# Seven products in one more place of a two-layer trunk, a pair of steps moved back by one, and a scaling deferred

## The chip, the cores and the metric

The kernel runs on one core of one Trainium2 chip. The metric is device time of one execution in microseconds (us). Three runs of the kernel before took 2038.50, 2039.89 and 2045.22 us, median 2039.89. The profiled execution is a separate one.

## The reference

Two layers over 256 tokens of width 2048, all in float32. Cut to what matters here:

```python
for l in range(DEPTH):                                   # 2 layers
    h = rms_norm(x, norm1_g[l]);  z = h @ w_in[l]        # 2048 -> 5120
    ...                                                  # 8 attention heads, 8 gated groups -> mix
    x = x + mix @ w_out[l]                               # 2048 -> 2048
    h2 = rms_norm(x, norm2_g[l])
    x = x + square(relu(h2 @ w_up[l])) @ w_down[l]       # 2048 -> 8192 -> 2048
return rms_norm(x, final_g)
```

The change touches only the last product of a layer, with `w_down`, and its result's way back to x.

## The kernel before

**Splitting.** A float32 product is made of three matmuls. Every weight tile arrives by DMA as `raw`; ScalarE (ACT) rounds it to `hi` (line 167), VectorE (DVE) makes `lo = raw - hi` (line 177). The activations are split in the same way (`to_half`, lines 640 and 643). TensorE (PE) then adds hi x hi, hi x lo and lo x hi.

**Steps.** The whole program is a list of steps, each with its weight units, its matmuls and what follows. An ordinary step (`transposed`, lines 400 to 404) takes one unit of 512 x 256 weights and issues 24 matmuls of 256 columns. The emission loop (lines 993 to 1014) goes through the list; `done` counts units, and at each step ACT is given the `hi` of units up to six ahead of `done`, VectorE the `lo` of units up to five ahead, then the step's matmuls are issued. Each engine works its own instructions in this order.

**The MLP in eighths.** The hidden width of 8192 is cut into eighths of 1024. The loop over e (lines 902 to 922) lines up, for e = 0 to 8, the sixteen ordinary steps of the up product of eighth e and then the steps of the down product of eighth e-1. The text calls one turn of it block e. The hidden values are squared without the norm's factor for e below 7; the results are scaled by the squared factor (`n2.r2`, `n2.R2`) when they go back into x.

**Seven products.** For some groups of 512 output columns the down product is done as two steps of `fast` instead of four ordinary steps: a 2 x 2 block product with seven multiplications in place of eight. One such step has four weight units: Top, Bottom, and two Sums, which VectorE makes in place from the raw tiles (lines 218, 219, 222, 223). It has 36 matmuls (lines 430, 432, 433) of six products; the seventh product's six matmuls are left over and go behind the third matmul of the next ordinary step. The step also needs sums of the hidden values: `sums` (lines 796 to 799 on VectorE) and four `parts`, each split by ACT and VectorE (lines 640, 643 with the tile `shared`), queued behind the last up step of the eighth. `sums_ready` issues what is still missing of them ahead of the step's matmuls. The seven accumulators of group 0 stay in PSUM (tile `aux`) over the blocks; those of groups 1 and 2 are copied out by ACT (lines 897, 883) and added up in DRAM by DMAs that POOL issues (`put`, line 862; tile `far`). In the last block of a group (`FINAL`) they come back, `combine` adds them to the four quarters on VectorE, ACT scales these by `n2.r2` (line 825), `turn_back` transposes them on TensorE (line 835), and `update` adds them to x (line 499).

**Order.** `ORDER` and `USUAL` give for each block and group the two indices among the block's ordinary steps ahead of which the two seven-product steps stand. `soon(n, fn)` calls fn at the first step at which `done` is n units further; `later` puts work into a queue of which each step takes about 1.2 units of cost. In block 1 today only groups 0 and 1 use seven products, at indices 7, 10 and 13, 14; the third group's columns (1024 to 1535) are four ordinary steps there, and `after_down` adds them to x directly (lines 761 and 499). In blocks 2 to 6 group 1 stands at 1, 2, group 2 at 6, 7 and group 0 at 11, 14.

Of the kernel before, what the change touches and what calls it, by code (L numbers as in the profile page):

```python
# [31 lines left out]
AF = mybir.ActivationFunctionType  # L32
OP = mybir.AluOpType
# [26 lines left out]

ORDER = {1: ((7, 10), (13, 14)), 7: ((6, 9), (1, 2)), 8: ()}
FINAL = (7, 7, 6)
LAST = (4, 6, 8, 10, 0, 2, 12, 14)
USUAL = ((11, 14), (1, 2), (6, 7))
WARM = 11
HALVES = 5
D_SCORES, D_NORM, D_TURN, D_VALUES = 2, 1, 3, 2
# [21 lines left out]
def trunk(ctx: ExitStack, tc: tile.TileContext, layout, xT, consts, gains, w, b_sp, w_sp, out):  # L91
    nc = tc.nc
# [10 lines left out]
    vec, act, pe = nc.vector, nc.scalar, nc.tensor  # L103
# [142 lines left out]
    def soon(delay, fn):  # L246

        due.append((now[0] + delay, fn))
# [258 lines left out]
    def layer(l, n1, n2, n3, last):  # L507
# [218 lines left out]
        d = 0  # L726
        if l == 0:
            d = 9
# [27 lines left out]
        def after_down(e, c, ps):  # L756

            if e == 8:
                update(n3, c, ps, True, last)
            elif c < 12:  # L760
                vec.tensor_tensor(pair(ps), pair(ps), wide(n2.R2), op=OP.mult)
                update(n3, c, ps, False, last)
            elif e == 1:
                act.activation(rest_sums[:, c - 12:c - 10, :], pair(ps), AF.Copy)
            else:
                y = rest_sums[:, c - 12:c - 10, :]
                vec.tensor_tensor(y, y, pair(ps), op=OP.add)
# [40 lines left out]
        def combine(place, c, banks, o=None):  # L808

            d1, d2, d3, d5, d7, d6, d4 = (place[:, 256 * n:256 * (n + 1)] for n in range(7))  # L810
            p1, p2, p3, p5, p7, p6, p4 = o or (d1, d2, d3, d5, d7, d6, d4)
            if o:
                act.activation(d1, p1, AF.Copy)
            vec.tensor_tensor(d2, d1, p2, op=OP.add)
            vec.tensor_tensor(d6, d1, p6, op=OP.add)
            vec.tensor_tensor(d7, d6, p7, op=OP.add)
            vec.tensor_tensor(d6, d6, p5, op=OP.add)
            vec.tensor_tensor(d3, d6, p3, op=OP.add)
            vec.tensor_tensor(d4, d7, d4, op=OP.subtract)
            if o:  # L820
                vec.tensor_tensor(d4, d4, p4, op=OP.subtract)
            vec.tensor_tensor(d7, d7, p5, op=OP.add)
            for tt, out in enumerate(((d2, d3), (d4, d7))):
                for d in out:
                    act.activation(d, d, AF.Copy, scale=n2.r2[:, tt:tt + 1])
            wait = 6 if o else 7
            soon(wait, lambda: turn_back(c, d2, d4, banks[0]))
            soon(wait + (1 if o else 2), lambda: turn_back(c + 2, d3, d7, banks[1]))

        def turn_back(c, first, second, bank):  # L830
            ps = bank()
            for j in range(2):
                for tt, src in enumerate((first, second)):
                    o = j * S + tt * P
                    pe.transpose(ps[:, o:o + P], src[:, j * P:(j + 1) * P], ident)
            soon(1, lambda: update(n3, c, ps, False, last))
# [20 lines left out]
        far = [dp.tile([P, 256 if g == 0 else 7 * 256], F32, name=f"far{l}{g}") for g in range(3)]  # L857

        def put(e, g, r):

            src = stage[:, r] if g else stage_one
            nc.gpsimd.dma_start(far[g][:, r], src, **({} if e == max(g, 1) else {"accum_op": OP.add}))  # L862

        def seventh_out(e, o):
            act.activation(stage_one, o[6], AF.Copy)  # L865
            put(e, 0, slice(0, 256))

        def first_done(e):
            def f(o):
                if e < 7:  # L870
                    soon(5, lambda: seventh_out(e, o))
                else:
                    soon(10, lambda: nc.gpsimd.dma_start(stage[:, 1536:1792], far[0]))
                    soon(14, lambda: combine(stage, 0, [aux_bank] * 2, o))
                    for i, c in enumerate((12, 14)):
                        soon(17 + 2 * i, lambda c=c: rest_in(c))
            return f

        def other_done(e, g, banks):
            here = [lambda i=i: acc_bank(i) for i in (2, 3)]  # L880

            def rest(o):
                act.activation(stage[:, 1536:1792], o[6], AF.Copy)
                for i in range(4):
                    soon(2 * i, lambda r=slice(512 * i, min(512 * (i + 1), 1792)): move(r))
                if e == FINAL[g]:
                    soon(9, lambda: combine(stage, 4 * g, here))

            def move(r):
                if e < FINAL[g]:  # L890
                    put(e, g, r)
                else:
                    nc.gpsimd.dma_start(stage[:, r], far[g][:, r], accum_op=OP.add)

            def f(o):
                for i in (2, 0, 1):
                    act.activation(stage[:, 512 * i:512 * (i + 1)], banks[i], AF.Copy)
                soon(5, lambda: rest(o))
            return f

        base = len(steps)
        for e in range(9):
# [3 lines left out]
            if e:  # L906
                w = 512 * len(ORDER.get(e, USUAL))
                hidden = [hid[e - 1]]
                down = collect(transposed, "w_down", l, (e - 1) * 1024, 8, w, D - w, from_tiles(hidden, NH),
                               lambda c, ps, e=e, w=w: after_down(e, (c + w) // P, ps),  # L910
                               apart=last and e == 8, of=2 if e < 8 else 4,
                               cols=None if e < 8 else [c * P for c in LAST])
                for g, at in enumerate(ORDER.get(e, USUAL)):
                    banks = []
# [107 lines left out]
    for c, w in [(0, 1), (1, 1)] + [(c, 2) for c in range(2, KC, 2)]:  # L1022
        r = slice(c, c + w)
# [38 lines left out]
```

## Time and profile before

| what | value |
|---|---|
| median of three runs | 2039.89 us (2038.50 to 2045.22) |
| profiled execution, its own time | 2044.94 us |
| its span, first to last instruction | 2042.6 us |
| granted TensorE clock, mean | 0.998 |
| TensorE matmul busy | 2027.5 us (99%), 16834 matmuls |
| VectorE busy | 1579.3 us (77%) |
| ScalarE busy | 1214.8 us (59%) |
| GpSimd busy | 156.8 us (8%) |

A matmul's end is modelled in the profile, so the busy share of TensorE doesn't tell how densely matmuls are issued; the number of matmuls in equal stretches does. L402 is line 402 of the kernel; `out<-in` names the tiles that an instruction writes and reads, and a bracket behind a row gives the idle time of the engine before it and what ended it.

### The profile page before, as it was taken

The page shows a single profiled execution, that of the slowest core. Times are in us where ns is not written, and L with a number is a line of the kernel's source. Part 1 is how long each engine was busy: PE and PEld are TensorE (multiplying, and loading weights), DVE is VectorE, ACT ScalarE, POOL GpSimd, SP SyncE. Part 2 cuts the span into 40 slices and gives each one's busy share as a digit, 9 for nine tenths or more (in the row PEclk, how much of TensorE's full clock was granted, in tenths as well). Part 3 has the DMA queues.
Part 4 walks back from the last instruction along what each step waited for, and adds up shares of the span by engine and source line. Part 5 has one row for each costly group of instructions (what it writes and reads, how often), then busy time and mean ns, then how long its engine had stood idle before and what let it go on. Part 6 is the DMA issues. An engine that isn't in the chain of part 4 may idle for free.

```text
span 2042.6 us, 40747 instructions
## 1 busy us (share of the span) xinstructions
PE 2027.5 (99%) x16834; PEld 1988.6 (97%) x16834; DVE 1579.3 (77%) x1950; ACT 1214.8 (59%) x1613; POOL 156.8 (8%) x200
## 2 busy tenths in 40 slices
PE   9999999999999999999999999999999999999997
PEld 8998999999999999999989989999999999999997
DVE  7566765788888888888855667667888888888985
ACT  7565455666675665765545554556665766667654
POOL 0002300001010010100000023000010100100000
PEclk9999999999999999999999999999999999999999
DMA  9555556567586776865565555555676866868562
GB/s 326 191 166 167 184 193 203 168 233 220 196 260 206 227 220 193 241 214 202 197 216 172 169 176 191 191 191 178 217 231 199 272 190 216 256 197 259 184 217 84
DMA packets 126442, 419.26 MB, mean 205 GB/s; under 512 B 14128, under 2 KB 22064, under 8 KB 126256
## 3 DMA queue, kind: packets, MB, share of 16 engines
q1 hardware_dynamic: 110800, 389.86, 56.3%
q0 software_dynamic: 14304, 23.86, 6.4%
q8 instruction: 131, 2.15, 0.4%
q10 hardware_dynamic: 1152, 2.94, 0.4%
q14 instruction: 55, 0.45, 0.1%
HBM read 394.58 MB, written 22.02 MB: 204 GB/s over the span
## 4 chain that ended last, share of the span: by engine, by line
PE 91%; DVE 5%; ACT 2%; issue 1%; DMA 1%; ACTq 0%; DVEq 0%; SPq 0%
PE acc L402 22%; PE acc L404 22%; PE acc L400 22%; PE acc L461 3%; PE acc L459 3%; PE acc L460 3%; PE aux L430 3%; PE aux L433 3%; PE aux L432 3%; PE acc L430 2%; PE acc L432 2%; PE acc L433 2%; DVE lo L177 2%; ACT hi L167 1%; DVE shared L643 1%
## 5 line engine op out<-in xcount | busy, mean ns | idle before, releaser
L167 ACT ACTIVATE hi<-raw 128x1024 fp32r<-128x1024 f32 (+1 forms) x817 | 836.8, 1050 | 516.2 <-DVE raw L219 233.9
L177 DVE TENSOR_TENSOR lo<-raw,hi 128x1024 fp32r<-128x1024 f32 (+1 forms) x817 | 965.0, 1213 | 155.8 <-ACT hi L167 153.6
L400 PE MATMUL acc<-hs,hi 128*128 128x256 f32 x2816 | 784.4, 279 | 0.0
L402 PE MATMUL acc<-hs,lo 128*128 128x256 f32 x2816 | 782.5, 278 | 0.4
L404 PE MATMUL acc<-hs,hi 128*128 128x256 f32 x2816 | 781.3, 277 | 0.0
L402 PEld LDWEIGHTS acc<-hs,lo 128*128 128x128 f32 x2816 | 529.2, 188 | 2.7 <-DVE lo L177 2.0
L400 PEld LDWEIGHTS acc<-hs,hi 128*128 128x128 f32 x2816 | 530.8, 189 | 0.4 <-issue 0.2
L404 PEld LDWEIGHTS acc<-hs,hi 128*128 128x128 f32 x2816 | 529.0, 188 | 0.0
L400 PE MATMUL acc<-half,hi 128*128 128x256 f32 x1344 | 373.0, 278 | 2.3 <-ACT hi L167 2.3
L402 PE MATMUL acc<-half,lo 128*128 128x256 f32 x1344 | 372.0, 277 | 0.0
L404 PE MATMUL acc<-half,hi 128*128 128x256 f32 x1344 | 372.0, 277 | 0.0
L400 PEld LDWEIGHTS acc<-half,hi 128*128 128x128 f32 x1344 | 252.8, 188 | 2.6 <-ACT hi L167 2.6
L402 PEld LDWEIGHTS acc<-half,lo 128*128 128x128 f32 x1344 | 252.6, 188 | 0.0
L404 PEld LDWEIGHTS acc<-half,hi 128*128 128x128 f32 x1344 | 252.4, 188 | 0.0
L862 POOL DMA_DIRECT2D far<-ar x92 | 74.7, 983 | 1168.2 <-ACT ar L865 620.7
L432 PE MATMUL acc<-lo,shared 128*128 128x256 f32 x384 | 107.4, 280 | 0.0
L433 PE MATMUL acc<-hi,shared 128*128 128x256 f32 x384 | 106.6, 277 | 0.0
L430 PE MATMUL acc<-hi,shared 128*128 128x256 f32 x384 | 106.5, 277 | 0.0
L643 DVE TENSOR_TENSOR half<-ar,half 128x512 fp32r<-128x512 f32 x72 | 49.7, 691 | 67.8 <-ACT half L640 67.6
L459 PE MATMUL acc<-hi,hs 128*128 128x512 f32 x256 | 101.7, 397 | 0.0
L461 PE MATMUL acc<-hi,hs 128*128 128x512 f32 x256 | 100.7, 393 | 0.0
L460 PE MATMUL acc<-lo,hs 128*128 128x512 f32 x256 | 100.0, 390 | 0.5 <-DVE lo L177 0.5
(163 smaller groups left out, 2563.3 us busy)
## 6 DMA issues: line engine op xcount, KB each, us to landing
raw<-in_w SPq DMA_DIRECT2D x731, 512.0 KB, 4.6
far<-ar POOLq DMA_DIRECT2D x60, 256.0 KB, 7.4
far<-ar POOLq DMA_DIRECT2D x32, 128.0 KB, 5.1
ar<-far POOLq DMA_DIRECT2D x12, 256.0 KB, 8.6
raw<-in_w SPq DMA_DIRECT2D x10, 256.0 KB, 4.8
x<-in_xT SPq DMA_DIRECT2D x7, 256.0 KB, 6.0
out<-x SPq DMA_DIRECT2D x7, 256.0 KB, 3.1
shared<-in_b_sp ACTq DMA_DIRECT2D x2, 512.0 KB, 7.7
```

Source lines behind the costliest of these rows:

```text
L167: act.activation(self.h[:, j * m:(j + 1) * m], self.raw[:, j * m:(j + 1) * m], AF.Copy)
L177: vec.tensor_tensor(lo[:, r], self.raw[:, r], self.h[:, r].bitcast(F32), op=OP.subtract)
L400: pe.matmul(o, lhsT=hi, rhs=xs[:, 0, :], start=(k0 + k == 0 and (two or cb == 0)), stop=False, skip_group_check=True)
L402: pe.matmul(o, lhsT=wt.lo[:, k, cb * P:(cb + 1) * P], rhs=xs[:, 0, :], start=False, stop=False, skip_group_check=True)
L404: pe.matmul(o, lhsT=hi, rhs=xs[:, 1, :], start=False, stop=last, skip_group_check=True)
L430: pe.matmul(o[n], lhsT=xh, rhs=hi, start=(p == 0 and k == 0 and n in fresh), stop=False, skip_group_check=True)
L432: pe.matmul(o[n], lhsT=xh, rhs=lo, start=False, stop=False, skip_group_check=True)
L433: pe.matmul(o[n], lhsT=xl, rhs=hi, start=False, stop=(n in last and p == 1 and k == 1), skip_group_check=True)
L459: pe.matmul(ps, lhsT=xh, rhs=hi, start=(k0 + k == 0), stop=False)
L460: pe.matmul(ps, lhsT=xh, rhs=lo, start=False, stop=False)
L461: pe.matmul(ps, lhsT=xl, rhs=hi, start=False, stop=(k0 + k == KC - 1))
L862: nc.gpsimd.dma_start(far[g][:, r], src, **({} if e == max(g, 1) else {"accum_op": OP.add}))
```

## The change

Three places change. `ORDER` loses its entry for block 1, which then follows `USUAL`: three groups use seven products there, with the pair of group 1 at 2, 3, that of group 2 at 6, 7 and that of group 0 at 11, 14. In `USUAL` and in block 7 the pair of group 1 moves from 1, 2 to 2, 3. The scaling in `combine` is no longer issued right behind VectorE's sums but by `soon(3, ...)`. With group 2 starting in block 1, `put` copies in block 1 and adds in all later ones, for every group.

```diff
-ORDER = {1: ((7, 10), (13, 14)), 7: ((6, 9), (1, 2)), 8: ()}
+ORDER = {7: ((6, 9), (2, 3)), 8: ()}
 FINAL = (7, 7, 6)
 LAST = (4, 6, 8, 10, 0, 2, 12, 14)
-USUAL = ((11, 14), (1, 2), (6, 7))
+USUAL = ((11, 14), (2, 3), (6, 7))
...
             vec.tensor_tensor(d7, d7, p5, op=OP.add)
-            for tt, out in enumerate(((d2, d3), (d4, d7))):
-                for d in out:
-                    act.activation(d, d, AF.Copy, scale=n2.r2[:, tt:tt + 1])
+
+            def scale():
+                for tt, out in enumerate(((d2, d3), (d4, d7))):
+                    for d in out:
+                        act.activation(d, d, AF.Copy, scale=n2.r2[:, tt:tt + 1])
+
+            soon(3, scale)
             wait = 6 if o else 7
...
-            nc.gpsimd.dma_start(far[g][:, r], src, **({} if e == max(g, 1) else {"accum_op": OP.add}))
+            nc.gpsimd.dma_start(far[g][:, r], src, **({} if e == 1 else {"accum_op": OP.add}))
```

## The prediction

> **What bounds the kernel now.** I read the page's first lines, then the waits of the weight load, then equal stretches of TensorE, then single matmuls where the stretches differ.
>
> ```profile
> span 2042.6 us, 40747 instructions
> PE 2027.5 (99%) x16834; PEld 1988.6 (97%) x16834; DVE 1579.3 (77%) x1950; ACT 1214.8 (59%) x1613; POOL 156.8 (8%) x200
> ...
> PEld acc L400 <- ACT hi L167: 2.6, 2, 1.3
> PEld acc L402 <- DVE lo L177: 2.0, 8, 0.3
> ```
>
> TensorE issues a matmul all the time, and its waits on others sum to a few us (the last two rows: total, times, longest). So the time is the number of matmuls times their spacing, plus few waits. The spacing has two values (columns: stretch, its length, then busy us and count of each engine, granted clock, DMA):
>
> ```profile
> 562.00:635.00 73.00, 73.00 (x644) 73.00 (x643) 62.64 (x72) 48.73 (x62) 7.54 (x9) 1.00 0.74 228
> 646.00:719.00 73.00, 73.00 (x623) 73.00 (x622) 61.06 (x70) 47.16 (x61) 7.39 (x9) 1.00 0.73 225
> 719.00:792.00 73.00, 73.00 (x623) 73.00 (x623) 60.92 (x65) 47.21 (x60) 7.89 (x9) 1.00 0.82 251
> 792.00:865.00 73.00, 73.00 (x624) 73.00 (x622) 64.84 (x78) 46.81 (x61) 7.08 (x8) 1.00 0.68 206
> 904.50:939.00 34.50, 34.50 (x295) 34.50 (x294) 32.09 (x39) 23.40 (x30) 3.55 (x4) 1.00 0.81 258
> ...
> 1661.00:1734.00 73.00, 73.00 (x644) 73.00 (x643) 62.75 (x72) 48.53 (x62) 7.23 (x9) 1.00 0.74 228
> ```
>
> (Block e is a turn of the loop over e, lines 902 to 922: the up product of eighth e and the down product of eighth e-1.) The same mix of work puts 644 matmuls into 73 us in one block (113.4 ns each) and 623 in another (117.2 ns) at the same granted clock of 1.00. I call them the quick and the slow rhythm. The slow one fills about 644 to 883 and 904 to 945 in layer 0, 280 us together, and costs 280/73 x 21 x 0.1134 = 9.1 us of this execution. Where does it begin? At waits in the seven-product steps (single matmuls: start, duration):
>
> ```profile
> 641.54 0.28 PE L433 MATMUL acc<-hi,shared 128*128 128x256 f32 x1
> 641.65 0.28 PE L430 MATMUL acc<-hi,shared 128*128 128x256 f32 x1
> 641.81 0.39 PE L432 MATMUL acc<-lo,shared 128*128 128x256 f32 x1
> 642.04 0.28 PE L433 MATMUL acc<-hi,shared 128*128 128x256 f32 x1
> ...
> 643.80 0.28 PE L433 MATMUL acc<-hi,shared 128*128 128x256 f32 x1
> 643.92 0.28 PE L400 MATMUL acc<-hs,hi 128*128 128x256 f32 x1
> 644.24 0.39 PE L402 MATMUL acc<-hs,lo 128*128 128x256 f32 x1
> 644.47 0.28 PE L404 MATMUL acc<-hs,hi 128*128 128x256 f32 x1
> ...
> 557.96 0.39 PE L432 MATMUL acc<-lo,shared 128*128 128x256 f32 x1
> ...
> 1909.60 0.39 PE L432 MATMUL acc<-lo,shared 128*128 128x256 f32 x1
> ...
> 1657.05 0.28 PE L433 MATMUL acc<-hi,shared 128*128 128x256 f32 x1
> ...
> 1658.75 0.28 PE L433 MATMUL acc<-hi,shared 128*128 128x256 f32 x1
> ```
>
> Ahead of 641.65 the starts lie 0.11 apart. The L432 of the fourth product waits for its low part, and from 642.04 to 643.80, 15 matmuls on, they lie 0.117 apart: the wait left the step in the slow rhythm. Eight such waits stand inside a seven-product step (the first and the last are the rows at 557.96 and 1909.60). Seven left it slow; the one at 1656.8 did not (1657.05 to 1658.75 is 0.113 each). Here a second wait follows at the ordinary step behind (643.92 to 644.47), and after most of these second waits the rhythm is quick again; after this one it wasn't. Once ordinary steps run slow, seven-product steps that end without a wait do not end it: the two slow stretches hold eighteen of them. Both ended where turned-back products are transposed:
>
> ```profile
> L835 PE MATMUL acc<-con,ar x32: 271/273/274, 876.4 to 1953.3; 128*128 128x128 f32 x32
> ```
>
> **Matmuls.** Per layer block 1 loses four ordinary steps of 24 matmuls and gains two seven-product steps of 42: 12 fewer, 24 in both layers, x 0.1134 = **-2.7 us**. VectorE gets, per new step, three low parts of 1.22, one of 0.68 and four sums of 0.69 (7.1 us beside 42 x 0.1134 = 4.8 us of TensorE), and loses per layer four low parts and the four operations that scaled and added columns 8 to 11 to x.
>
> ```profile
> L177 DVE TENSOR_TENSOR lo<-raw,hi 128x1024 fp32r<-128x1024 f32 x807 | 958.4, 1220 | 151.9 <-ACT hi L167 149.7
> L190 DVE TENSOR_TENSOR lo<-raw,hi 128x512 fp32r<-128x512 f32 x76 | 52.0, 684 | 1.3 <-ACT hi L185 1.3
> L218 DVE TENSOR_TENSOR raw<-raw 128x512 f32<-128x512 f32 x76 | 52.0, 684 | 0.0
> L862 POOL DMA_DIRECT2D far<-ar x92 | 74.7, 983 | 1168.2 <-ACT ar L865 620.7 <-ACT ar L897 436.7 <-ACT ar L883 110.8
> ```
>
> So 14.2 - 4.9 - 2.8 = 6.5 us more on VectorE in a block of 83 us; the blocks that already do this keep it 62.64 of 73 us busy. On average it is hidden; where it isn't comes next. POOL issues four more transfers a layer (0.98 us each), and those of block 2 add instead of copy; POOL idles 1168 us ahead of this line and the next access to the same place is a block later: nothing. Uncovered, they would be 8 us on POOL's own queue, on which nothing of TensorE waits.
>
> **The new first pair.** In block 1 the first pair now sits behind the second ordinary step instead of the seventh. Between it and the last up step of block 0, whose output the sums are made of, no down steps lie. The order in which VectorE gets its work up to the third step is by the code the same as before, so its rows of today hold:
>
> ```profile
> 379.79 0.69 DVE L643 TENSOR_TENSOR half<-ar,half 128x512 fp32r<-128x512 f32 x1 [2.35 <-ACT half L640]
> 380.52 0.69 DVE L796 TENSOR_TENSOR ar<-ar 128x512 f32<-128x512 f32 x1
> ...
> 384.44 1.28 DVE L643 TENSOR_TENSOR shared<-ar,shared 128x512 fp32r<-128x512 f32 x2
> 385.64 1.22 DVE L177 TENSOR_TENSOR lo<-raw,hi 128x1024 fp32r<-128x1024 f32 x1
> 386.78 1.28 DVE L643 TENSOR_TENSOR shared<-ar,shared 128x512 fp32r<-128x512 f32 x2
> ...
> 377.63 0.28 PE L400 MATMUL acc<-hs,hi 128*128 128x256 f32 x1
> ...
> 383.07 0.28 PE L400 MATMUL acc<-hs,hi 128*128 128x256 f32 x1
> ...
> 384.66 0.28 PE L404 MATMUL acc<-hs,hi 128*128 128x256 f32 x1
> ```
>
> Block 1's first step starts at 377.63, its third at 383.07: there the pair's first step will start. Its first two products (12 matmuls) need only the hidden tile; the third reads the low part of sum rows 4 and 5, at matmul 14, that is 384.66. VectorE makes that part in the first half of the row at 386.78, done 387.4. TensorE waits **2.8 us**, in both layers (layer 1 has the same rows 1015.0 us later): **+5.6 us**. Queued behind it are only matmuls, and VectorE uses the pause to get ahead, so the second of the pair follows without one. Bounds: 0, if the parts were made in another order; 3.4, if the step waits for the last part (the row's end, 388.06).
>
> **The later pair elsewhere.** Blocks 3 to 6 now wait twice around the pair: 0.05 + 0.12 inside it and 0.21 + 0.11 behind it by the rows from 641.65 to 644.47, 0.49 together. One ordinary step more ahead of the pair gives 24 x 0.1134 = 2.72 us for 1.22 us of VectorE, 1.5 us of lead, more than the 0.49: gone in six such places (blocks 3 and 4 of layer 0, whose 5 and 6 ran slow and had none, and four in layer 1): **-2.9 us**. The pair's evacuation by ACT and its four transfers on POOL follow a step later, and SP loads the same tiles in the new order; POOL is idle and seven raw buffers stand between: nothing. The next pair keeps its place; work and time ahead of it are unchanged in sum, so its lead stays. In block 7 VectorE works without a pause up to the other pair, so a wait removed early can come back there: between 0 and 1.3 us, I take **-0.6**.
>
> **The scaling.** ACT now stands before it while VectorE combines; the question is whether TensorE feels it.
>
> ```profile
> L825 ACT ACTIVATE ar<-ar,nr 128x256 f32<-128x256 f32 x24 | 10.9, 500 | 9.1 <-DVE ar L814 5.1 <-DVE ar L818 3.4 <-DVE ar L821 0.6
> ...
> 970.14 0.69 DVE L761 TENSOR_TENSOR acc<-acc,nR 128x512 f32<-128x512 f32 x1
> 970.87 0.69 DVE L499 TENSOR_TENSOR x<-x,acc 128x512 f32<-128x512 f32 x1
> ...
> 970.28 0.28 PE L404 MATMUL acc<-half,hi 128*128 128x256 f32 x1
> 971.70 0.36 PE L400 MATMUL acc<-half,hi 128*128 128x256 f32 x1 [1.15 <-ACT hi L167]
> ```
>
> TensorE's longest wait after the start is here, 1.3 us in each layer. The row blames ACT, but this matmul opens a bank which VectorE's L499 has to free, and that ends at 971.56. The combine's sums stay ahead of it, so deferring ACT's scaling changes nothing: **0**. If the row is right, -2.6. A loss needs the scaling to come too late for the transposes: it still has at least one ordinary step (2.72 us) for its four operations (2.0 us).
>
> **What follows the new wait.** It is a wait inside a seven-product step, like the eight, and no wait comes at the step behind it to mend the rhythm. By those rows it runs slow, and stays slow up to the transposes late in block 6 (876.4 today). A block has 20 x 24 + 6 x 42 = 732 matmuls, 732 x 3.8 ns = 2.8 us; 0.9 of block 1, four whole ones and 0.9 of block 6 make 16.2 us a layer, **+32.4**. Bounds: 0 and 32.4. I take the upper, by seven of eight. The Trainium skill (TensorE: Matmul & The Clock Gate, "Step-by-step: what each phase is for") says that loading the next weights takes no read bandwidth from the running matmul; by it a wait would cost its own length and no more. The 623 against 644 matmuls disagree, though they don't show why. That rule's result is the first rival below.
>
> Sum, on the profiled execution's 2044.94 us (span 2042.6): -2.7 + 5.6 - 2.9 - 0.6 + 0 - 9.1 (today's slow stretches, begun by waits that go) + 32.4 = **2067.6 us**. The median of the runs, 2039.89, lies 5 us under the profiled execution; without a slow rhythm today's kernel would take 2035.8, so I read the median as 4 us of it. Against the median the forecast is 1.4% slower.
>
> **Rivals.** *The rhythm stays quick* behind the new wait: 2067.6 - 32.4 = 2035.2. For it: the one quick case in eight, and that the wait is far longer than those. Against: the other seven. *One layer only* goes slow: 2051.4; the same kernel shows both rhythms in layer 0 and only the quick one in layer 1, so chance decides. *On the other side, the new pair does not wait*: it is decided by whether the low part of sum rows 4 and 5 lands by 384.6 rather than 387.4. VectorE stands idle 2.35 us ahead of 379.79, so there is room; but the row after must wait for the last up step, and then nothing is idle. Then neither wait nor slow rhythm: 2035.2 - 5.6 = 2029.6, 0.5% faster. *The change of ACT's order does what I deny*, with a quick rhythm: 2035.2 - 2.6 = 2032.6.
>
> **How the numbers follow.** What a measurement can tell from no change is 0.3%, 6.1 us: 2033.8 to 2046.0. Forecast 0.38, one layer 0.16, quick rhythm 0.18 (two thirds of it inside the 0.3%, the rest faster), no wait 0.15, ACT's order 0.09, something slower of another kind 0.04. Faster: 0.15 + 0.09 + 0.06 = 0.30; same 0.12; slower 0.58. The range goes from 2031 (leaving out the no-wait case) to 2071 (the longer wait and no gain at the pairs); the forecast's own range is 2060 to 2071.
>
> **What would show it.** Right: a TensorE wait near 2.8 us in the third product after two ordinary steps of block 1, ended by VectorE's L643, in both layers; 623 matmuls per 73 us from there to the transposes; none of the 0.1 to 0.3 us waits for L177 at the pair in later blocks; 16810 matmuls; the 1.3 us wait in the last down block but one still there. Wrong: 644 matmuls per 73 us after that wait, or no wait.

## The result, and the profile after

The changed kernel takes 2058.36 us (median of 4 runs, 2055.94 to 2058.51) beside 2039.2 us for the kernel before on the same chip: 1.0088 times as long (the ratio is taken over all runs, not of the medians), 95% interval 1.0072 to 1.0103. The forecast was 1.4% slower: 2067.6 us for the profiled execution, which took 2058.51, below the forecast's own range of 2060 to 2071. Sign and first cause are as predicted. Most of the difference is lost at steps that the prediction had counted as unchanged or as a small gain, and its largest term, a slow rhythm behind the new wait, is missing.

The page of the changed kernel (first lines: span, then busy us, share and count of each engine) and its waits of TensorE (total, times, longest):

```profile
span 2056.7 us, 40733 instructions
PE 2030.9 (99%) x16810; PEld 1986.4 (97%) x16810; DVE 1593.3 (77%) x1966; ACT 1225.9 (60%) x1629; POOL 163.7 (8%) x208
...
PE acc L402 <- DVE lo L177: 5.7, 14, 1.3
PE acc L433 <- DVE shared L643: 4.0, 2, 2.0
...
PE acc L430 <- ACT shared L640: 0.8, 2, 0.4
```

TensorE has the 24 matmuls fewer that the diff promises (16834 before), and three waits that the kernel before did not have in this view. The last two rows are the new first pair of block 1 (behind the edit, line numbers from 826 on are 4 higher; line 897 is now 901, line 883 is 887). Its matmuls in layer 0, and the same place in layer 1 (start, duration, and in brackets the idle time and what ended it):

```profile
385.11 0.39 PE L430 MATMUL acc<-hi,shared 128*128 128x256 f32 x1 [0.41 <-ACT shared L640]
385.34 0.28 PE L432 MATMUL acc<-lo,shared 128*128 128x256 f32 x1
387.63 0.38 PE L433 MATMUL acc<-hi,shared 128*128 128x256 f32 x1 [2.02 <-DVE shared L643]
387.85 0.28 PE L430 MATMUL acc<-hi,shared 128*128 128x256 f32 x1
...
1402.51 0.38 PE L433 MATMUL acc<-hi,shared 128*128 128x256 f32 x1 [2.02 <-DVE shared L643]
...
1402.99 0.41 PE L433 MATMUL acc<-hi,shared 128*128 128x256 f32 x1
1403.21 0.42 PE L430 MATMUL acc<-hi,shared 128*128 128x256 f32 x1
...
1405.98 0.41 PE L432 MATMUL acc<-lo,shared 128*128 128x256 f32 x1
1406.20 0.34 PE L433 MATMUL acc<-hi,shared 128*128 128x256 f32 x1
1406.38 0.28 PE L430 MATMUL acc<-hi,shared 128*128 128x256 f32 x1
```

Four starts lie later than 0.113 behind the one before them, 2.97 us in all, in each layer. In layer 1 something follows that was not foreseen: for 3.2 us the starts lie 0.213 apart. That is not the slow rhythm (0.117) but half speed, and the granted clock (0.76 over 1402 to 1409) says so; it costs 1.7 us. The stretches of the changed kernel (length, then busy us and count of each engine, granted clock, DMA):

```profile
420.00:493.00 73.00, 73.00 (x644) 73.00 (x644) 60.88 (x69) 47.97 (x62) 5.37 (x8) 1.00 0.69 228
589.00:662.00 73.00, 73.00 (x644) 73.00 (x643) 61.66 (x72) 47.12 (x61) 7.02 (x8) 1.00 0.72 226
758.00:831.00 73.00, 73.00 (x644) 73.00 (x643) 61.74 (x71) 47.12 (x61) 7.03 (x8) 1.00 0.72 227
1402.00:1409.00 7.00, 6.49 (x42) 6.50 (x43) 6.84 (x10) 2.40 (x3) 0.00 (x0) 0.76 0.25 87
1437.00:1510.00 73.00, 73.00 (x623) 73.00 (x622) 59.59 (x67) 46.01 (x59) 5.36 (x8) 1.00 0.68 222
1524.00:1597.00 73.00, 73.00 (x644) 73.00 (x643) 62.18 (x71) 47.13 (x60) 6.86 (x9) 1.00 0.74 227
1777.00:1850.00 73.00, 73.00 (x623) 73.00 (x622) 60.84 (x69) 45.03 (x57) 6.70 (x8) 1.00 0.73 224
```

Layer 0 is quick (644) all the way behind the new wait. In layer 1 the rhythm is quick too from 1408 on, as soon as the half speed is over; the slow rhythm (623) fills 1435 to 1514 and 1775 to 1854, 158 us, not the 1000 us forecast: 158/73 x 21 x 0.1134 = 5.2 us. Both stretches begin at waits of the pair of group 2, not at the new first pair.

The waits for L177 are where most of the rest is. They no longer stand at the first pair but at the second one (group 2, ahead of the steps 6 and 7), in blocks 1 to 6. TensorE, ACT and VectorE in block 3, around that pair:

```profile
566.40 0.28 PE L433 MATMUL acc<-hi,shared 128*128 128x256 f32 x1
566.51 0.28 PE L400 MATMUL acc<-hs,hi 128*128 128x256 f32 x1
...
579.49 0.28 PE L400 MATMUL acc<-hs,hi 128*128 128x256 f32 x1
580.03 0.38 PE L402 MATMUL acc<-hs,lo 128*128 128x256 f32 x1 [0.26 <-DVE lo L177]
```

```profile
566.71 1.58 ACT L901 ACTIVATE ar<-acc 128x512 f32<-128x512 f32 x3 [2.13 <-PE acc L433]
568.16 1.07 ACT L167 ACTIVATE hi<-raw 128x1024 fp32r<-128x1024 f32 x1
...
573.67 1.07 ACT L167 ACTIVATE hi<-raw 128x1024 fp32r<-128x1024 f32 x1 [2.98 <-DVE raw L219]
574.64 0.58 ACT L780 ACTIVATE ar<-acc 128x512 f32<-128x512 f32 x1
...
577.67 1.05 ACT L167 ACTIVATE hi<-raw 128x1024 fp32r<-128x1024 f32 x1
...
569.27 1.23 DVE L177 TENSOR_TENSOR lo<-raw,hi 128x1024 fp32r<-128x1024 f32 x1 [3.05 <-ACT hi L167]
...
577.53 2.44 DVE L177 TENSOR_TENSOR lo<-raw,hi 128x1024 fp32r<-128x1024 f32 x2 [0.26 <-ACT hi L167]
```

The first pair's last matmul starts at 566.40. Only when it ends does ACT begin to copy the banks out (1.58 us), and the next high part, which VectorE has been idle 3.05 us for, stands behind the copies. From there the work is one chain: high part, three low parts and VectorE's sums of the weight tiles, a high part of those sums, ACT's part of the up product (L780 and behind), two more high parts, and the low part for L402, which is done at 577.53 + 2.44 = 579.97. That is 13.3 us from the pair's end (566.68). TensorE reaches the L402 13.1 us after the pair (566.51 to 579.60) and waits 0.43 us. Smaller waits follow right behind it, in the pair's second step and in the ordinary step after that, so that each block loses 0.43 + 0.11 + 0.06 + 0.11 + 0.19 + 0.11 = 1.0 us; blocks 1 to 6 of both layers lose 11.2 together (blocks 2 and 6 of layer 1, which TensorE goes through in the slow rhythm, 0.6 each). The same chain in the kernel before:

```profile
560.27 1.58 ACT L897 ACTIVATE ar<-acc 128x512 f32<-128x512 f32 x3 [0.43 <-PE acc L433]
...
562.83 2.36 DVE L177 TENSOR_TENSOR lo<-raw,hi 128x1024 fp32r<-128x1024 f32 x2 [1.35 <-ACT hi L167]
...
572.50 2.36 DVE L177 TENSOR_TENSOR lo<-raw,hi 128x1024 fp32r<-128x1024 f32 x2 [0.26 <-ACT hi L167]
```

There it takes 574.86 - 560.27 = 14.6 us, one low part more, but four ordinary steps stand between the pairs and not three: 13.1 + 2.72 = 15.8 us of cover, 1.2 to spare.

Block 7, where group 0 comes next behind the first pair, waits too:

```profile
918.81 0.38 PE L402 MATMUL acc<-hs,lo 128*128 128x256 f32 x1 [0.24 <-DVE lo L177]
...
933.37 0.39 PE L402 MATMUL acc<-hs,lo 128*128 128x256 f32 x1 [1.32 <-DVE lo L177]
```

With the smaller waits around them that is 2.5 us a layer, 5.0 in both.

The sum from the profiled execution before (2044.94) to the one after (2058.51, 13.6 more), in us: matmuls -2.7; new first pair +5.9; half clock +1.7; second pair +11.2; block 7 +5.0; waits at the first pair that went -4.3; slow rhythm -9.1 + 5.2. These make +12.9; the other 0.7 is not placed.

### The profile page after: what moved, and what is told of

The parts are those of the page before. It is cut to its first block, busy times and chain, and to the rows that moved or that the text cites. A ratio compares the mean times of both kernels' runs of the same rounds, so it can differ in the third digit from the quotient of the medians.

```text
span 2056.7 us, 40733 instructions
## 1 busy us (share of the span) xinstructions
PE 2030.9 (99%) x16810; PEld 1986.4 (97%) x16810; DVE 1593.3 (77%) x1966; ACT 1225.9 (60%) x1629; POOL 163.7 (8%) x208
## 4 chain that ended last, share of the span: by engine, by line
PE 89%; DVE 5%; ACT 4%; issue 2%; ACTq 0%; DVEq 0%
PE acc L402 21%; PE acc L404 21%; PE acc L400 21%; PE acc L432 3%; PE acc L459 3%; PE acc L460 3%; PE acc L461 3%; PE acc L433 3%; PE acc L430 3%; PE aux L430 2%; PE aux L433 2%; PE aux L432 2%; ACT hi L167 2%; DVE lo L177 2%; ACT ar L901 1%
## 5 line engine op out<-in xcount | busy, mean ns | idle before, releaser
L167 ACT ACTIVATE hi<-raw 128x1024 fp32r<-128x1024 f32 (+1 forms) x821 | 845.3, 1051 | 524.5 <-DVE raw L219 241.2
L177 DVE TENSOR_TENSOR lo<-raw,hi 128x1024 fp32r<-128x1024 f32 (+1 forms) x821 | 970.7, 1214 | 159.2 <-ACT hi L167 156.2
L402 PE MATMUL acc<-hs,lo 128*128 128x256 f32 x2816 | 782.2, 278 | 6.0 <-DVE lo L177 5.7
L402 PEld LDWEIGHTS acc<-hs,lo 128*128 128x128 f32 x2816 | 528.8, 188 | 11.6 <-DVE lo L177 11.1
L400 PE MATMUL acc<-half,hi 128*128 128x256 f32 x1280 | 354.8, 277 | 2.3 <-ACT hi L167 2.3
L402 PE MATMUL acc<-half,lo 128*128 128x256 f32 x1280 | 353.8, 276 | 0.0
L404 PE MATMUL acc<-half,hi 128*128 128x256 f32 x1280 | 353.8, 276 | 0.0
L400 PEld LDWEIGHTS acc<-half,hi 128*128 128x128 f32 x1280 | 240.6, 188 | 2.6 <-ACT hi L167 2.6
L404 PEld LDWEIGHTS acc<-half,hi 128*128 128x128 f32 x1280 | 240.4, 188 | 0.0
L402 PEld LDWEIGHTS acc<-half,lo 128*128 128x128 f32 x1280 | 240.3, 188 | 0.0
L866 POOL DMA_DIRECT2D far<-ar x100 | 81.5, 986 | 1181.3 <-ACT ar L901 747.8
L433 PE MATMUL acc<-hi,shared 128*128 128x256 f32 x416 | 116.2, 279 | 4.0 <-DVE shared L643 4.0
L432 PE MATMUL acc<-lo,shared 128*128 128x256 f32 x416 | 117.3, 282 | 0.0
L430 PE MATMUL acc<-hi,shared 128*128 128x256 f32 x416 | 116.1, 279 | 0.8 <-ACT shared L640 0.8
L643 DVE TENSOR_TENSOR half<-ar,half 128x512 fp32r<-128x512 f32 x72 | 49.7, 691 | 66.1 <-ACT half L640 66.1
```

The costliest lines, as they stand in the source:

```text
L167: act.activation(self.h[:, j * m:(j + 1) * m], self.raw[:, j * m:(j + 1) * m], AF.Copy)
L177: vec.tensor_tensor(lo[:, r], self.raw[:, r], self.h[:, r].bitcast(F32), op=OP.subtract)
L400: pe.matmul(o, lhsT=hi, rhs=xs[:, 0, :], start=(k0 + k == 0 and (two or cb == 0)), stop=False, skip_group_check=True)
L402: pe.matmul(o, lhsT=wt.lo[:, k, cb * P:(cb + 1) * P], rhs=xs[:, 0, :], start=False, stop=False, skip_group_check=True)
L404: pe.matmul(o, lhsT=hi, rhs=xs[:, 1, :], start=False, stop=last, skip_group_check=True)
L430: pe.matmul(o[n], lhsT=xh, rhs=hi, start=(p == 0 and k == 0 and n in fresh), stop=False, skip_group_check=True)
```

## The experiments

"Before" is the kernel before on the same chip in each case; ratios are to it, with 95% intervals. The profiled time is the execution that the trace shows.

**Which edit costs what.** The scaling alone, and the pair's place alone:

```diff
 scale_only: the kernel before, with only
+            soon(3, scale)
 pair_move_only: the kernel before, with only
-ORDER = {1: ((7, 10), (13, 14)), 7: ((6, 9), (1, 2)), 8: ()}
+ORDER = {1: ((7, 10), (13, 14)), 7: ((6, 9), (2, 3)), 8: ()}
-USUAL = ((11, 14), (1, 2), (6, 7))
+USUAL = ((11, 14), (2, 3), (6, 7))
```

> The kernel before with ACT's scaling deferred, nothing else. The prediction's reading: no change, 2036 to 2042 us, and the 1.3 us wait in the down steps of block 7 still there, because VectorE frees the bank late. Rival (the row that blames ACT is right): that wait goes in both layers, 2.6 us less.

> The kernel before with the first pair at 2, 3 in blocks 2 to 7, nothing else (block 1 keeps two groups). The prediction's claim: the waits at the first pair go and the second pair keeps its lead: 2039.2 - 3.5 = 2035.7 us. Distance theory: 1.0 us of waits appear at the second pair of blocks 2 to 6 and 2.5 us at group 0's steps in block 7, 10 + 5 - 4.3 = 10.7 us more: 2046 to 2051 us.

The scaling: 2037.45 us beside 2037.76, 0.9994 [0.9985, 1.0004], with the same waits, also the 1.3 us one in the down steps of block 7, which the row blames on ACT (its 2.3 are one of 1.1 in each layer, as the row counts idle time):

```profile
PE acc L400 <- ACT hi L167: 2.3, 2, 1.1
```

So its 0 was right. The pair's move: 2050.55 us (2047.97 to 2052.72), 1.0062 [1.0047, 1.0077], where the prediction's -2.9 and -0.6 would have made it faster. In the profile (2052.72) the waits at the first pair are gone and those at the second pair of blocks 2 to 6 and in block 7 stand as in the changed kernel:

```profile
PE acc L402 <- DVE lo L177: 5.2, 12, 1.3
```

The move, which the forecast counted as a gain, costs about 13 us by itself. In the profiled execution the waits make some 10 us more; 213 us of slow rhythm, which begin at waits of the second pair, make another 7 us.

**Is it the distance between the pairs?** The pair after the first is brought nearer instead, and in another kernel block 7 alone is set back:

```diff
 near_pairs: the kernel before, with only
-USUAL = ((11, 14), (1, 2), (6, 7))
+USUAL = ((11, 14), (1, 2), (5, 6))
 block7_back: the changed kernel, with only
-ORDER = {7: ((6, 9), (2, 3)), 8: ()}
+ORDER = {7: ((6, 9), (1, 2)), 8: ()}
```

> The kernel before with the second pair at 5, 6 instead of 6, 7 in blocks 2 to 6; the first pair stays at 1, 2. So the pairs are three ordinary steps apart, as in the changed kernel, without moving the first. If the lead is reset behind the first pair, the second pair's waits are those of the changed kernel, 1.0 us in ten blocks: 2037.8 + 10 = 2048 us. If lead is carried over from pair to pair, they are larger by the 1.5 us that the first pair lacks: about 2.5 us, 2063 us. If distance doesn't matter: 2038.

> The changed kernel with block 7 as before (6, 9 and 1, 2). The 2.5 us of waits at group 0's two steps go and the 0.5 to 0.8 us at the first pair come back: 2058.4 - 3.7 = 2054.7 us. If those waits come from elsewhere: 2058.

Nearer: 2054.3 us, 1.0076 [1.0059, 1.0093]. With the first pair where it was before, the second waits 1.2 us a block in blocks 3 to 6, and the first pair's 0.5 us remains. So the time between the pairs decides: the first pair's place, one step earlier than in the changed kernel, alters little (1.2 us for 1.0, not the 2.5 of a lead that is carried over). The profiled execution, quick but for 36 us in block 7, takes 2050.55, which is about 2037.8 and the new waits of both layers, 2 x (4 x 1.2 + 1.5) = 12.6 (block 2 waits 1.5); the median lies 4 us higher, in executions that were not profiled. Block 7 set back: 2053.5 us, 1.0071 [1.0056, 1.0086]; its 2.5 us a layer are gone, and small waits of 0.8 to 1.0 us a layer stand in their place, as in the kernel before (0.7 and 1.0).

**The new first pair of block 1**, put later:

```diff
 first_pair_later2: the changed kernel, with
-ORDER = {7: ((6, 9), (2, 3)), 8: ()}
+ORDER = {1: ((13, 15), (5, 6), (9, 10)), 7: ((6, 9), (2, 3)), 8: ()}
```

> The changed kernel, with block 1's groups at 5, 6 then 9, 10 then 13, 15. If the first pair's wait is a price of its own, its 2.97 us in each layer and the halved clock behind it in layer 1 (1.7 us) go: 2050.8 us, with the second pair's waits in block 1 as they were, and up to 1 us a layer more at 13 and 15, which stand closer than 11 and 14 did. If VectorE is overloaded by the third group: above 2055.

2051.39 us, 1.0060 [1.0045, 1.0075]: the 2.97 us wait and the half clock behind it are gone in both layers, and block 1 has smaller waits of the pair and of group 0 in its place. Two earlier kernels of this kind put group 0's second step behind the last up step (index 17), and so compute with the next eighth's sums and wait for them: `first_pair_later` with ((14, 17), (5, 6), (9, 10)) in block 1, 2068.95 us, and `second_pair_later` with ((14, 17), (2, 3), (9, 10)) in all usual blocks, 2150.87. Their times answer nothing here. One row of the second is still of use: in its trace, with six ordinary steps between the pairs, no L402 waits for L177 at the second pair of blocks 1 to 6. This fits the distance, but does not prove it, since group 0's new waits of some 5 to 6 us a block give VectorE time as well.

> The changed kernel, with block 1's three groups at 5, 6 then 9, 10 then 14 and 17; all else as changed. If the first pair's wait is a price of its own (2.97 us in each layer, and 1.7 us of halved clock in layer 1), it goes and nothing comes in its place: 2058.4 - 7.6 = 2050.8 us, the 1.0 us at the second pair still there in blocks 1 to 6. If VectorE is simply overloaded by the third group, the wait comes back in other steps of block 1: above 2055 us.

> The changed kernel with the second pair at 9, 10 and group 0 at 14, 17 (blocks 1 to 6). Distance theory: ACT's copying out of the first pair's banks holds back the next high parts, so the lead ahead of the second pair is made only in the ordinary steps between them; with six of them instead of three the 1.0 us of waits per block go, 11.6 us in all, and a slow rhythm begun there too: 2042 to 2047 us. Overload theory (too much VectorE work per block, wherever it stands): 2055 us or more.

**Which work makes the low part late?** Two of ACT's three copies are put off, first by two units, then by five, the latter also in the kernel before:

```diff
 split_copies: the changed kernel, with
-                for i in (2, 0, 1):
-                    act.activation(stage[:, 512 * i:512 * (i + 1)], banks[i], AF.Copy)
+                def out(i):
+                    act.activation(stage[:, 512 * i:512 * (i + 1)], banks[i], AF.Copy)
+                out(2)
+                soon(2, lambda: (out(0), out(1)))
 late_copies: the same with soon(5, ...); late_copies_alone: that in the kernel before
```

> The changed kernel; of the three banks that ACT copies out behind a pair, only the one that is needed next is copied at once, the other two some units later. Same steps at the same places. Distance theory (ACT's copies hold back the high parts, VectorE stands idle and its lead is lost): ACT is free 1.05 us earlier, so the 1.0 us of waits at the second pair of blocks 1 to 6 fall by more than half, 2048 to 2053 us against 2058.4. Overload theory: no change, 2056 to 2060.

> The changed kernel, whose two copies by ACT of the banks that the next steps do not need come five units later, so behind the high part of the unit whose low part the second step of the second pair waited for. Theory that ACT's order of work behind the first pair makes that low part late: the 1.0 us per block at the second pair fall below 0.3 us in blocks 1 to 6 of both layers and the 0.8 us at the first step of group 0 in block 7 goes: 2058 less 8 to 13, that is 2045 to 2050. Rival, that VectorE simply has too much work between two pairs so near to each other: the waits stay at 1.0 us per block, 2056 to 2058. Second rival, that the two copies then delay the high parts behind them: the wait moves to the ordinary steps behind the second pair, with the same size, and the time stays too.

> The kernel before, with only these two copies five units later. If they are what eats the lead, its own waits at the first pair of blocks 2 to 6, some 0.5 us each, shrink also: 2037.6 less up to 5, 2033 to 2037. If those waits come from the group 0 steps that stand 2 and 5 steps ahead of the first pair, which copy out nothing in that way, nothing changes: 2037 to 2039. If the copies come to stand in front of work that matters more, it is slower than 2039.

Two units: 2054.28 us, 1.0075 [1.0060, 1.0090]; where the rhythm is quick, the waits at the second pair are unchanged to 0.01 us, against the expectation; only those at the first step of group 0 in block 7 went (0.9 us a layer). The copies now stand behind one high part and ahead of L780: a seven-product step counts four units, so two units are over at the next step. Wherever they stand in the chain, they add the same. Five units: 2080.67 us, 1.0205 [1.0187, 1.0223], which none of the three theories gave. The late low part no longer shows, but the next pair's first matmul opens a bank that isn't copied out yet (waits, then one of the twelve):

```profile
PE acc L430 <- ACT ar L901: 15.7, 12, 1.5
```

```profile
582.37 0.39 PE L430 MATMUL acc<-hi,half 128*128 128x256 f32 x1 [1.48 <-ACT ar L901]
```

At about 1.6 us each that is 19.3 us in place of 11.2; the rest of the loss is the slow rhythm, some 700 us of it (23 us by the same sum as above). This wait would have hidden the late low part in any case, so the run does not say where the copies should stand, and in the kernel before nothing changes: 2039.81 us beside 2039.24, 1.0003 [0.9995, 1.0012].

What would tell is a shorter chain. VectorE idles for 3.05 us just then, so it gets the two copies, of the first pair only:

```diff
 copies_by_vectore: the changed kernel, with
                 for i in (2, 0, 1):
-                    act.activation(stage[:, 512 * i:512 * (i + 1)], banks[i], AF.Copy)
+                    if g == 1 and i != 2:
+                        vec.tensor_copy(stage[:, 512 * i:512 * (i + 1)], banks[i])
+                    else:
+                        act.activation(stage[:, 512 * i:512 * (i + 1)], banks[i], AF.Copy)
```

> The changed kernel, in which VectorE instead of ACT copies out two of the three banks of the first pair (group 1) only. In the changed kernel VectorE stands idle for 3.05 us per block behind that pair, because ACT's three copies (1.58 us) wait for the pair's end and the next high part stands behind them. Theory of the one serial chain (pair's end, ACT's copies, a high part, VectorE's low parts and sums, the next high part, and so on to the second pair's low parts, 13.3 us against 13.0 us of matmuls that cover it): the two copies go into VectorE's idle time, the chain gets 1.0 us shorter, the waits of 1.0 us per block at the second pair fall to 0.2 us or less in blocks 1 to 6 of both layers: 2058 less 8 to 13, 2045 to 2050. Rival, that VectorE has too much work between two pairs so near to each other: 1.4 us more work for it, the waits grow by that much a block: 2065 to 2075.

The same place of block 3 (the DVE row of L902 is the second of its two copies), then the waits, then the stretches:

```profile
564.53 0.60 ACT L904 ACTIVATE ar<-acc 128x512 f32<-128x512 f32 x1 [2.13 <-PE acc L433]
...
563.41 0.68 DVE L902 COPY ar<-acc 128x512 f32<-128x512 f32 x1
...
574.37 2.45 DVE L177 TENSOR_TENSOR lo<-raw,hi 128x1024 fp32r<-128x1024 f32 x2 [0.26 <-ACT hi L167]
...
577.43 0.28 PE L402 MATMUL acc<-hs,lo 128*128 128x256 f32 x1
```

```profile
PE acc L433 <- DVE shared L643: 4.0, 2, 2.0
PE acc L402 <- DVE lo L177: 2.5, 2, 1.3
```

```profile
589.00:662.00 73.00, 73.00 (x644) 73.00 (x643) 65.11 (x75) 45.75 (x58) 5.32 (x7) 1.00 0.74 228
...
1524.00:1597.00 73.00, 73.00 (x623) 73.00 (x622) 63.57 (x74) 43.55 (x54) 5.11 (x6) 1.00 0.70 218
1693.00:1766.00 73.00, 73.00 (x623) 73.00 (x622) 63.60 (x74) 44.37 (x56) 5.11 (x6) 1.00 0.71 218
1820.00:1893.00 73.00, 73.00 (x624) 73.00 (x623) 66.73 (x78) 47.38 (x59) 6.93 (x8) 1.00 0.71 214
```

The low part lands at 576.82, 0.6 us ahead of its L402 where it was 0.37 late: 1.0 us gained, the duration of the two copies that left ACT (1.58 - 0.60). The waits at the second pair are gone but for one of 0.4 us and five under 0.1 in layer 0; the two of 1.3 us left under L402 are block 7's. With 1.4 us more work a block VectorE is not late: the chain, not the amount, made the wait. Yet the time is 2062.84 us (2050.64 to 2074.03), 1.0122 [1.0081, 1.0162], and not 2045 to 2050: now the predicted slow rhythm is there. In layer 1 it starts at the new wait of block 1, behind 2.8 us of half speed, and lasts to the transposes of block 6 (1399 to 1902): 503/73 x 21 x 0.1134 = 16.4 us. Layer 0 is quick but for 4 us behind that wait. The profiled execution took 2055.79; with both layers slow it would be 2072, and the six runs lie at 2050.6 to 2055.8 and at 2069.9 to 2074.0. That the upper ones have both layers slow is read from the times alone; they were not profiled.

The rows show one thing more. VectorE has made both copies by 563.41 + 0.68 = 564.09, 0.4 us before ACT can begin with the third (564.53): the pair's last products go into the third bank alone, so the other two are complete earlier. ACT idles 2.13 us just there in both kernels, because its order (2, 0, 1) begins with the bank that is finished last. Copying the other two first might shorten the chain without VectorE; no run tried it, and the bank that is copied first now is the one that the next step needs.

**Is there a better place for the third group?** The kernel before, with the third group in block 1 but four ordinary steps between the pairs:

```diff
 third_group_far: the kernel before, with the change's line in put, and
-ORDER = {1: ((7, 10), (13, 14)), 7: ((6, 9), (1, 2)), 8: ()}
+ORDER = {1: ((14, 15), (5, 6), (10, 11)), 7: ((6, 9), (1, 2)), 8: ()}
```

> The kernel before with the third group of block 1 as seven products, in the order that leaves four ordinary steps between the two pairs (the sums' pair before the steps 5 and 6, the second pair before 10 and 11, group 0 before 14 and 15), and no other pair moved, no scaling moved. Theory of the distance: no new wait of the second pair above 0.5 us, no wait for the sums, 2.7 us less work on TensorE: 2035 to 2038 beside 2037.6. Rival, that a block with all three groups as seven products has too little room whatever the order: 1 to 3 us of waits in each block 1, 2039 to 2042.

2038.03 us beside 2039.24, 1.0007 [0.9991, 1.0023]: no difference that can be told. There is no wait above 0.1 us at the two pairs of block 1, as the distance theory says, but group 0's steps right behind them wait 1.0 us a layer, so 2.0 of the 2.7 us are given back. Here too the slow rhythm runs through a layer when it is not ended: from 446, at a wait in group 0's last step of block 1, through layer 0 of the profiled execution (2049.8 us; eight of the twelve runs lie between 2036.9 and 2038.5):

```profile
465.00:538.00 73.00, 73.00 (x623) 73.00 (x622) 61.56 (x66) 47.84 (x61) 7.92 (x9) 1.00 0.79 244
...
810.00:883.00 73.00, 73.00 (x624) 73.00 (x623) 63.82 (x73) 48.63 (x64) 7.96 (x9) 1.00 0.76 239
```

## Why the prediction was right or wrong

**Matmuls, -2.7:** right, 16810 of them; but `third_group_far` shows how little such a gain is worth next to one wait a block.

**The new first pair, +5.6:** right in place, cause and size: 2.97 us a layer for 2.8, in the third product, ended by VectorE's L643. Not foreseen were that its first 0.6 us wait for ACT's half of the same split (L640), and the clock behind it in one layer, +1.7.

**The later pair, -2.9:** the half that it looked at was right; the waits at the first pair are gone, -4.3 with block 7. The step that failed is the sentence "The next pair keeps its place; work and time ahead of it are unchanged in sum, so its lead stays." Sums over the block do not matter, because a lead does not pass a pair: ACT's copies start when the pair's matmuls end, the next high part is behind them in ACT's queue, and VectorE idles until it comes (3.05 us after the change, 1.35 before: the lead gained ahead of the pair is idled away there). What counts is the chain from one pair's end against the steps up to the next. That is 13.3 against 13.1 us where it had been 14.6 against 15.8. The cost was +11.2. `pair_move_only` and `near_pairs` show that the distance decides, `copies_by_vectore` that the chain through ACT's copies is what is too long for it. The idle time of VectorE ahead of L177 (1.35 us) was in the trace of before; the prediction did not read it as the end of a lead.

**Block 7, -0.6:** wrong for the same reason, group 0's steps being the next ones there: +5.0 for the waits themselves. `block7_back` takes them away.

**The scaling, 0:** right (`scale_only`).

**Today's slow stretches, -9.1:** they went, but against the median this was never a gain of that size: most of the later runs of before lie between 2037 and 2040, so by their times they have little of it, and the profiled one had much.

**The slow rhythm behind the new wait, +32.4:** wrong in the changed kernel. The prediction had named the sign of it: 644 matmuls per 73 us behind that wait. Neither layer of the profiled execution went slow there; the 5.2 us of slow rhythm begin later, at waits of the second pair. That such a wait can start a slow rhythm up to block 6 holds, and its size a layer too (16.4 us for 16.2 in `copies_by_vectore`). Two premises failed. The wait starts it less often than seven times in eight: over the changed kernel and the four experiments that keep this wait, it lasted past the pair in 6 of 10 layers (the changed kernel's two are among the other four). And "no wait comes at the step behind it to mend the rhythm" left out the waits that the change itself brings: in `split_copies`, `block7_back` and `late_copies` the slow stretch that the first pair began ended at a wait of the second pair or of the banks, some 25 to 115 us on. Where these waits were removed (`copies_by_vectore`), it ran to block 6 in the one layer in which it lasted. So even where the rhythm goes slow, the change's own new waits cut it short. That the total is only 9 us off is luck: a term of 32.4 us that did not come and some 18 us of waits and half speed that were not forecast, with 5.2 us of slow rhythm from elsewhere, stand against each other.

Of the rivals, "the rhythm stays quick" (2035.2) had the rhythm behind the new wait right in both layers and missed the 18 us of other new waits and half speed.

## What to carry to other kernels

When a step is moved, do not balance work against time over the whole loop: find where a lead is thrown away (an evacuation that must wait for the last matmul, with the next input's preparation in the same queue behind it) and compare the serial chain from there with the matmuls up to the next step that needs its result. An idle engine just behind such a point is the sign. Work in that chain costs the same wherever it stands in it; it must leave the queue, not move within it.

## What the runs showed of the hardware that was not expected

**Half clock after a broken wait.** In 6 of 10 layers with the new wait, matmuls behind it ran 0.213 us apart for 2.8 to 3.2 us; the stretch of 7 us shown above has a granted clock of 0.76. The Trainium skill (TensorE: Matmul & The Clock Gate, "🔬 Part 1: The HAM clock gate") says that the clock halves after at least one idle window of about 3.4 us, on windows that run freely. Here 2.97 us sufficed, and with two matmuls inside: the rows show idle times of 0.41 and 2.02 us. That some layers show it and others not fits free-running windows; that a full window of idleness is needed does not fit.

**A rhythm that waits start and end.** Ordinary steps at 1.00 granted clock run at 113.4 or 117.2 ns a matmul; a wait inside a seven-product step can start the slow one, and a wait at or in a later step can end it, as can the transposes. What sets it inside TensorE stays open; the runs only show where it changes.
